# A tile's small product ahead of the next tile's transposes, two norm weights loaded as rows with the taps, and four raw buffers for the small columns

## The chip, the cores and the metric

The kernel runs on one core of one Trainium2 chip. The metric is device time in microseconds (us) of one execution; lower is better. Engines are named as the profile names them: PE (TensorE matmuls and transposes; PEld its weight loads), DVE (VectorE), ACT (ScalarE), POOL (GpSimd), SP (the queue that issues most DMAs).

## The reference

One layer of a hybrid decoder block, float32, on 1024 tokens of width 1024. Only what the change touches is followed closely below: the norm of the input, the narrow ("small") columns of the input projection, and the two norm weights of the sparse attention.

```python
h = rms_norm(x, norm_mix)                          # x (1024, 1024)
proj = h @ w_in                                    # w_in (1024, 3020)
qkv, z, a_g, b_g, c_q, c_kv, k_idx, w_idx, ug = split_cols(proj, IN_SPLITS)
y_a = gdn_mixer(qkv, z, a_g, b_g, ...)             # causal conv of 4 taps, gated delta rule in chunks
y_b = dsa_mixer(c_q, c_kv, k_idx, w_idx, ..., dsa_q_norm, dsa_k_norm)   # top-k sparse attention
y_c = conv_mixer(ug, ...)                          # causal conv of 31 taps, layer norm
x = x + concat([y_a, y_b, y_c]) @ w_out
x = x + memory_cross_attention(rms_norm(x, norm_cross), rms_norm(mem, norm_mem), ...)
x = x + square(relu(rms_norm(x, norm_mlp) @ mlp_w1)) @ mlp_w2
```

The 460 columns 2048 to 2507 of `w_in` (`a_g`, `b_g`, `c_q`, `c_kv`, `k_idx`, `w_idx`) are the small columns. In the sparse attention q and k are normed over 64 columns with the weights `dsa_q_norm` and `dsa_k_norm`, 64 numbers each.

## The kernel before

Tokens are worked in eight tiles of 128 rows. A float32 product is made from three products of rounded parts (`mm3`, L130 to L135): each operand is split into a high part, cast to fp32r, and a low part, the difference. `unit` (L170) loads a piece of a weight into a raw buffer, casts the high part on ACT or POOL and subtracts for the low part on DVE or POOL (L184). `split` (L142 to L145) does the same for an activation: the cast on ACT, the difference on DVE.

The program begins with `norm_small` (L290), and this is the part that the change is about. Four units of the small columns' weight are loaded (`ws`, two blocks of 128 rows of `w_in` each, here called u0 to u3); their raw buffers are the shared `wraw`, of which there are two. For u0 and u2 the low part is made on DVE, for u1 and u3 on POOL. Then a software pipeline runs over the tiles: at turn i it norms tile i (`rms_rows`: the squares and their sum on ACT, then a chain of ten short DVE instructions for the inverse root, L156 to L168; `norm_rows`: one DVE instruction of 1024 columns, L195), transposes tile i-1 on PE and splits it into `hT` (`rows_T`, 8 transposes, two casts on ACT, two differences on DVE), multiplies tile i-2 by the small columns (24 PE instructions of 460 columns into one bank of PSUM, then copies out), and does three later steps for tiles i-3, i-4 and i-5 (transposes of the small columns, `prep_tile`, `prep_queries`). The loads of x go into a pool of three buffers.

Written order is not final order: the program is built with a scheduler that moves instructions within each engine's queue by its own estimate of times. An engine then takes its queue strictly in order. So a change near the start can change the order of instructions far behind it.

`taps` (L681) gathers the convolutions' taps and two norm weights as rows of one tile and transposes it once on PE. `prep_keys` (L462), called after it, loads `dsa_q_norm` and `dsa_k_norm` as columns with four DMAs of 64 rows of one number and multiplies the two on DVE (`gqkc`, L472). After `norm_small` follow `ug_stage` (PE products of the columns of the convolution), the index scores and the top-k search, the qkv products with their convolution, the z gate, then a weave of the memory's keys and values (`mem_stage`, tiles `mkv`), the convolution's norm (`cyc`) and the first chunk of the delta rule (`gdn_pre`, `gdn_blocks`, `gdn_post`, tiles `gp`, `Tb`/`Wb`, `gi`), a weave of the eight chunks with the sparse attention (`da`), cross attention, and the MLP, which takes the second half of the time.

## Time and profile before

| | |
|---|---|
| median of three runs | 1643.58 us (1643.33 to 1648.39) |
| the profiled execution's own time | 1641.49 us |
| its span, from the first to the last instruction | 1639.7 us |
| busy share of the span | PE 93%, PEld 77%, DVE 72%, ACT 45%, POOL 20% |
| chain that ended last, by engine | PE 60%, DVE 18%, ACT 10%, issue 6%, DMA 4%, POOL 2% |
| mean granted TensorE clock | 0.963 of full speed |

Times in all rows count from the start of the span. The chain that ended last is followed back from the last instruction: at each step to what released it. A busy PE is not a PE at its peak.

### The profile page before, as it was taken

How to read it: one execution, taken by the hardware profiler on the slowest of the kernel's cores; microseconds unless marked ns; L12 is line 12 of the kernel's file. 1: busy time of each engine (PE TensorE's matmuls, PEld its weight loads, DVE VectorE, ACT ScalarE, POOL GpSimd, SP SyncE). 2: the span in 40 equal slices, each digit the busy share in tenths (PEclk: the TensorE clock that was granted, in tenths of full speed). 3: DMA queues.
4: the chain of work that ended last, by engine and by line, in shares of the span. 5: the costliest groups of instructions: out<-in, count | busy, mean ns of one | idle time of the engine just before them, and what ended most of it. 6: DMA issues, size and time to landing. Idle time of an engine off the chain costs nothing.

```text
span 1639.7 us, 20580 instructions
## 1 busy us (share of the span) xinstructions
PE 1519.0 (93%) x7497; PEld 1265.0 (77%) x7497; DVE 1174.4 (72%) x2149; ACT 740.2 (45%) x1483; POOL 322.4 (20%) x297
## 2 busy tenths in 40 slices
PE   6999999997985789999889997999999999999998
PEld 5977888885775678889777885788888888888887
DVE  7649868778158598886756878997569656965783
ACT  4535777883541456655434524433234223323331
POOL 3021434345355233221401104100000000000000
PEclk9999999998987799999999998999999999999999
DMA  5130121221543434322831347733560364146202
GB/s 188 58 99 19 44 62 52 78 71 43 158 138 110 145 103 124 100 72 82 293 112 39 123 173 272 307 113 116 196 227 26 131 231 177 52 154 238 96 7 97
DMA packets 114123, 201.93 MB, mean 123 GB/s; under 512 B 15469, under 2 KB 64358, under 8 KB 106854
## 3 DMA queue, kind: packets, MB, share of 16 engines
q1 hardware_dynamic: 112486, 195.37, 34.7%
q0 software_dynamic: 1536, 5.24, 0.9%
q8 instruction: 59, 0.97, 0.2%
q14 instruction: 42, 0.34, 0.1%
HBM read 150.26 MB, written 50.33 MB: 122 GB/s over the span
## 4 chain that ended last, share of the span: by engine, by line
PE 60%; DVE 18%; ACT 10%; issue 6%; DMA 4%; POOL 2%; SPq 0%; ACTq 0%; DVEq 0%; POOLq 0%
PE mlp_mm L135 12%; PE mlp_mm L134 12%; PE mlp_mm L133 12%; ACT junka L591 5%; DVE acc L739 1%; DVE bm L1454 1%; PE xw_mm L135 1%; PE xw_mm L134 1%; PE xw_mm L133 1%; PE xq_mm L135 1%; PE xq_mm L133 1%; DVE tk_t L599 1%; PE xq_mm L134 1%; DVE junk L593 1%; DVE Tb L994 1%
## 5 line engine op out<-in xcount | busy, mean ns | idle before, releaser
L134 PE MATMUL mlp_mm<-bm,wm 128*128 128x512 f32 x448 | 178.3, 398 | 5.9 <-DVE bm L1454 5.9
L135 PE MATMUL mlp_mm<-bm,wm 128*128 128x512 f32 x448 | 178.1, 398 | 0.3 <-DVE wm L1454 0.3
L133 PE MATMUL mlp_mm<-bm,wm 128*128 128x512 f32 x448 | 176.7, 397 | 1.2 <-ACT bm L1453 1.2
L134 PE MATMUL mlp_mm<-wm,am 128*128 128x512 f32 x448 | 176.9, 395 | 0.0
L135 PE MATMUL mlp_mm<-wm,am 128*128 128x512 f32 x448 | 176.9, 395 | 0.0
L133 PE MATMUL mlp_mm<-wm,am 128*128 128x512 f32 x448 | 175.0, 395 | 0.0
L1453 ACT CAST wm<-wq 128x2048 fp32r<-128x2048 f32 x32 | 61.2, 1911 | 212.2 <-PE mlp_mm L134 212.0
L1543 DVE TENSOR_TENSOR xacc<-xacc,mlp_mm 128x512 f32<-128x512 f32 x112 | 75.8, 682 | 69.5 <-PE mlp_mm L135 69.5
L134 PEld LDWEIGHTS mlp_mm<-bm,wm 128*128 128x128 f32 x448 | 84.8, 189 | 27.1 <-DVE bm L1454 6.7
L133 PEld LDWEIGHTS mlp_mm<-bm,wm 128*128 128x128 f32 x448 | 84.6, 189 | 21.8 <-ACT bm L1453 1.4
L135 PEld LDWEIGHTS mlp_mm<-bm,wm 128*128 128x128 f32 x448 | 84.9, 189 | 21.1 <-DVE wm L1454 0.8
L133 PEld LDWEIGHTS mlp_mm<-wm,am 128*128 128x128 f32 x448 | 84.2, 188 | 20.3
L134 PEld LDWEIGHTS mlp_mm<-wm,am 128*128 128x128 f32 x448 | 84.2, 188 | 20.2
L135 PEld LDWEIGHTS mlp_mm<-wm,am 128*128 128x128 f32 x448 | 84.2, 188 | 20.2
L1454 DVE TENSOR_TENSOR wm<-wsum,wm 128x2048 fp32r<-128x2048 f32 x24 | 58.2, 2427 | 52.3 <-ACT wm L1453 52.3
L1454 DVE TENSOR_TENSOR wm<-wq,wm 128x2048 fp32r<-128x2048 f32 x32 | 73.3, 2291 | 28.5 <-ACT wm L1453 28.4
L1453 ACT CAST wm<-wsum 128x2048 fp32r<-128x2048 f32 x24 | 45.9, 1912 | 105.9 <-PE mlp_mm L134 76.5
L1507 ACT ACTIVATE aq<-mlp_mm 128x512 f32<-128x512 f32 x64 | 37.9, 596 | 68.8 <-PE mlp_mm L135 68.6
L184 POOL TENSOR_TENSOR wlo<-wraw,whi 128x1024 fp32r<-128x1024 f32 x28 | 68.4, 2443 | 1.8
L133 PE MATMUL cv_mm<-Y,diag 128*128 128x512 f32 x124 | 50.2, 405 | 10.4 <-POOL diag L782 10.4
L591 ACT ACTIVATE junka<-negm,tk_cand 128x384 bf16<-128x384 int16 (+1 forms) x68 | 52.6, 774 | 15.1 <-DVE tk_cand L600 13.7
L591 ACT ACTIVATE junka<-lo,tk_cand 128x384 bf16<-128x384 uint16 (+1 forms) x64 | 49.5, 773 | 18.5 <-DVE tk_cand L600 12.5
(511 smaller groups left out, 4119.2 us busy)
## 6 DMA issues: line engine op xcount, KB each, us to landing
bm<-hb_d SPq DMA_DIRECT2D x42, 1024.0 KB, 5.8
wq<-in_mlp_w SPq DMA_DIRECT2D x32, 1024.0 KB, 5.3
hb_d<-bm SPq DMA_DIRECT2D x14, 1024.0 KB, 5.0
wraw<-in_w_in SPq DMA_DIRECT2D x20, 512.0 KB, 3.7
qkv_d<-acc SPq DMA_DIRECT2D x12, 512.0 KB, 3.2
x<-in_x SPq DMA_DIRECT2D x8, 512.0 KB, 6.4
gnx<-qkv_d SPq DMA_DIRECT2D x8, 512.0 KB, 3.9
wraw<-in_xa_wkv SPq DMA_DIRECT2D x8, 512.0 KB, 4.4
```

Source lines behind the costliest of these rows:

```text
L133: mm(out, l[0], r[0], start=start, stop=False, skip_group_check=on)
L134: mm(out, l[0], r[1], start=False, stop=False, skip_group_check=on)
L135: mm(out, l[1], r[0], start=False, stop=stop, skip_group_check=on)
L184: (lo_eng or nc.gpsimd).tensor_sub(lo[:, :n], raw[:, :n], hi[:, :n].bitcast(F32))
L591: Sc.activation(junka[:, :K], X[b], AF.Sign, bias=c, scale=-1.0, accum_out=n)
L593: V.tensor_scalar(junk[:, :K].bitcast(X[b].dtype), X[b], c, None, op0=OP.is_lt, op1=OP.add, accum_out=n)
L599: V.tensor_tensor(t, cnt, th, op=OP.is_le)
L739: nc.vector.scalar_tensor_tensor(acc, xb[:, 3 - d:3 - d + T], self.cw[:, 3 - d, i:i + 1], acc, op0=OP.mult, op1=OP.add)
L1453: Sc.copy(w[0], x)
L1454: V.tensor_sub(w[1], x, w[0].bitcast(F32))
L1507: Sc.activation(x, ps[ch, m], AF.Relu if c == "21" else AF.Copy)
L1543: V.tensor_add(x, x, ps[ch, tt])
```

## The change

Three edits. The two raw buffers that u2 and u3 had to share with u0 and u1 are no longer needed: u2 and u3 load into one `whi` and one `wlo` buffer of the same pool, and the loads of x tiles 1 and 2 are placed after u1 and after u3. In a turn of the pipeline the small product (of tile i-2) is written ahead of the transposes (of tile i-1). And the two attention norm weights become two more rows of the taps' tile, so the four column loads and their tile go away.

```diff
-        raw = (rpool or pool).tile([P, rcap or cap], F32, name=rtag or tag + "raw", bufs=raw_bufs)
+        rtag = rtag or tag + "raw"
+        raw = (rpool or pool).tile([P, rcap or cap], F32R if rtag in ("whi", "wlo") else F32, name=rtag, bufs=raw_bufs).bitcast(F32)
...
-                               rpool=wu, rtag="wraw", rcap=1024, hi_act=True, lo_eng=nc.vector if u % 2 == 0 else None))
-            if u < 2:
-                load(u + 1)
+                               rpool=wu, rtag=("wraw", "wraw", "whi", "wlo")[u], rcap=1024, hi_act=True, lo_eng=nc.vector if u % 2 == 0 else None))
+            if u == 1:
+                load(1)
+        load(2)
...
-            t = i - 1
-            if 0 <= t < NT:
-                self.stage = "n1"
-                sl = slice(t * P, (t + 1) * P)
-                self.rows_T(ys.pop(t), *((lambda q, m=m: m[:, q * 4:q * 4 + 4, sl]) for m in hT))
             t = i - 2
             if 0 <= t < NT:
                 self.stage = "small"
...
                 nc.vector.tensor_copy(ga[:, t, 8:12], ps[:, 456:460])
+            t = i - 1
+            if 0 <= t < NT:
+                self.stage = "n1"
+                sl = slice(t * P, (t + 1) * P)
+                self.rows_T(ys.pop(t), *((lambda q, m=m: m[:, q * 4:q * 4 + 4, sl]) for m in hT))
...
-        gc = pool.tile([P, 2], F32, name="gqc")
-        for j, nm in enumerate(("dsa_q_norm", "dsa_k_norm")):
-            for s in range(2):
-                src = A[nm]
-                nc.sync.dma_start(gc[s * 64:(s + 1) * 64, j:j + 1],
-                                  bass.AP(tensor=src.tensor, offset=src.offset, ap=[[1, 64], [1, 1]]))
+        gc = self.gqk
...
-        rows = pool.tile([121, P], F32, name="taprows")
+        rows = pool.tile([123, P], F32, name="taprows")
...
+        for i, nm in enumerate(("dsa_q_norm", "dsa_k_norm")):
+            src = A[nm]
+            nc.sync.dma_start(rows[121 + i:122 + i, :].rearrange("p (s n) -> p s n", s=2),
+                              bass.AP(tensor=src.tensor, offset=src.offset, ap=[[64, 1], [0, 2], [1, 64]]))
```

What the scheduler makes of it is seen in the queues. SP, from the program's start: the names are tiles with their buffer numbers; the four 128x2x460 loads are u0 to u3, the 128x1024 loads of `in_x` are the tiles of x. Before:

```order
L302 DMA x1_119<-in_x 128x1024
L140 DMA g1_121<-in_norm_mix 128x1024
L179 DMA wraw_123<-in_w_in 128x2x460
L302 DMA x1_129<-in_x 128x1024
L179 DMA wraw_131<-in_w_in 128x2x460
L302 DMA x1_137<-in_x 128x1024
...
L302 DMA x1_286<-in_x 128x1024
L469 DMA gqc_1124<-in_dsa_k_norm 64x1
L179 DMA wraw_139<-in_w_in 128x2x460
...
L179 DMA wraw_145<-in_w_in 128x2x460
```

After:

```order
L303 DMA x1_119<-in_x 128x1024
L140 DMA g1_121<-in_norm_mix 128x1024
L180 DMA wraw_123<-in_w_in 128x2x460
L180 DMA wraw_129<-in_w_in 128x2x460
L303 DMA x1_135<-in_x 128x1024
L180 DMA whi_137<-in_w_in 128x2x460
L180 DMA wlo_143<-in_w_in 128x2x460
L303 DMA x1_149<-in_x 128x1024
```

u1 moved ahead of x tile 1, u2 and u3 from far behind the taps to the places ahead of x tile 2, which goes from sixth to eighth.

PE, from the program's start: `n1_y_168`, `n1_y_188` and `n1_y_222` are the normed tiles 0, 1 and 2, of each of which four transposes at a time go into a bank; `small_mm` is the product, whose 24 rows are cut to the first and the last. Before:

```order
L202 MATMUL n1_mm_215<-ident_66,n1_y_168 128x128 x4
L202 MATMUL n1_mm_242<-ident_66,n1_y_188 128x128 x4
...
L133 MATMUL small_mm_256<-wshi_124,hT0_104 128x460
...
L135 MATMUL small_mm_256<-wshi_146,hT1_105 128x460
L202 MATMUL n1_mm_308<-ident_66,n1_y_222 128x128 x4
...
L133 MATMUL small_mm_322<-wshi_124,hT0_104 128x460
```

After:

```order
L203 MATMUL n1_mm_215<-ident_66,n1_y_168 128x128 x4
L133 MATMUL small_mm_242<-wshi_124,hT0_104 128x460
...
L135 MATMUL small_mm_242<-wshi_144,hT1_105 128x460
L203 MATMUL n1_mm_272<-ident_66,n1_y_188 128x128 x4
...
L133 MATMUL small_mm_308<-wshi_124,hT0_104 128x460
L134 MATMUL small_mm_308<-wslo_125,hT0_104 128x460
L203 MATMUL n1_mm_338<-ident_66,n1_y_222 128x128 x4
...
L350 MATMUL small_mm_352<-ident_66,sm_267 128x128 x4
L135 MATMUL small_mm_308<-wshi_124,hT1_105 128x460
```

Tile 0's whole product now stands ahead of tile 1's transposes; the first two instructions of tile 1's product stand ahead of tile 2's transposes, the other 22 behind them.

From the end of `norm_small` to the weave of memory and first chunk, some 390 us on, the queues of PE and POOL hold the same instructions in the same order; from there to the end of the sparse attention the scheduler's order differs again, and the MLP's is the same. POOL in that weave (`whi`, `wlo` are the parts of a unit of the memory's weight, `XT` begins the first chunk's `gi` steps). Before:

```order
L184 TENSOR_TENSOR wlo<-wraw,whi 128x1024
L833 TENSOR_TENSOR cyc<-cyc,conv_ln_b 128x1024
L183 TENSOR_SCALAR whi<-wraw 128x1024
L184 TENSOR_TENSOR wlo<-wraw,whi 128x1024
L183 TENSOR_SCALAR whi<-wraw 128x1024
L184 TENSOR_TENSOR wlo<-wraw,whi 128x1024
L1245 DMA gz<-gz_d 128x512 x2
L967 MEMSET Wb 32x272
L1014 TENSOR_TENSOR XT<-xc,bm 128x512
```

After:

```order
L835 TENSOR_TENSOR cyc<-cyc,conv_ln_b 128x1024 x2
L185 TENSOR_TENSOR wlo<-wraw,whi 128x1024
L184 TENSOR_SCALAR whi<-wraw 128x1024
L185 TENSOR_TENSOR wlo<-wraw,whi 128x1024
L1247 DMA gz<-gz_d 128x512 x2
L969 MEMSET Wb 32x272
L184 TENSOR_SCALAR whi<-wraw 128x1024
L1016 TENSOR_TENSOR XT<-xc,bm 128x512
L970 MEMSET Wb 32x16
L185 TENSOR_TENSOR wlo<-wraw,whi 128x1024
```

SP's queue keeps this weave's instructions but moves the last unit's load (`wraw<-in_xa_wkv`) from ahead of a `yc_d` store and the second load of `Ab` to just behind them. The last unit's two instructions moved from ahead of the clearing of `Wb` to either side of `XT`; in PE's queue 22 of that unit's products now stand between the first chunk's `gi_mm<-X,NAT` and its `gi_mm<-Z,XT`, where none stood.

## Rows read from the trace of the kernel before

**Rows 1.** Busy time by stretch: the stretch, its length, then for each engine busy us and, in brackets, instructions; then the granted PE clock, the DMA engines' mean busy share and GB/s.

```profile
27.00:76.00 49.00, 49.00 (x297) 45.13 (x295) 35.22 (x112) 24.86 (x63) 8.38 (x7) 1.00 0.29 92
76.00:87.00 11.00, 7.92 (x56) 6.76 (x54) 8.06 (x24) 9.51 (x28) 0.23 (x2) 0.93 0.34 100
560.00:780.00 220.00, 200.48 (x1426) 180.83 (x1425) 177.82 (x571) 134.36 (x351) 56.14 (x68) 0.98 0.32 98
```

**Rows 2.** Timeline of the first 28 us, PE: start, duration, engine, line, operation, output and input, shapes; in brackets how long the engine sat idle before it and what ended that.

```profile
16.49 1.97 PE L202 MATMUL n_mm<-ident,n_y 128*128 128x128 f32 x8 [5.48 <-DVE rs_i L158]
...
19.03 0.59 PE L135 MATMUL small_mm<-wshi,hT 128*128 128x460 f32 x1
19.41 0.59 PE L133 MATMUL small_mm<-wshi,hT 128*128 128x460 f32 x1
...
20.99 0.37 PE L135 MATMUL small_mm<-wshi,hT 128*128 128x460 f32 x1
21.20 0.37 PE L133 MATMUL small_mm<-wshi,hT 128*128 128x460 f32 x1
...
24.34 0.48 PE L134 MATMUL small_mm<-wslo,hT 128*128 128x460 f32 x1 [0.90 <-POOL wslo L184]
...
26.34 1.09 PE L202 MATMUL n_mm<-ident,n_y 128*128 128x128 f32 x8 [0.69 <-DVE rs_x L156]
```

**Rows 3.** Timeline of SP's queue: the issues of u1, u2 and u3 (the duration is that of the issue, not of the transfer).

```profile
2.70 0.43 SPq L179 DMA_DIRECT2D wraw<-in_w_in  x1
...
14.21 0.53 SPq L179 DMA_DIRECT2D wraw<-in_w_in  x1
...
15.37 0.53 SPq L179 DMA_DIRECT2D wraw<-in_w_in  x1
```

**Rows 4.** Timeline of ACT: the squares of x tile 1, the cast of u1, the two casts of tile 0's `hT`, the casts of u2 and u3.

```profile
9.15 1.06 ACT L191 ACTIVATE n_y<-x 128x1024 f32<-128x1024 f32 x1 [0.36 <-DMA x<-in_x]
...
10.41 0.96 ACT L181 CAST wshi<-wraw 128x920 fp32r<-128x920 f32 x1
...
11.28 1.06 ACT L144 CAST hT<-n_mm 128x512 fp32r<-128x512 f32 x2
...
19.39 0.96 ACT L181 CAST wshi<-wraw 128x920 fp32r<-128x920 f32 x1 [5.91 <-DMA wraw<-in_w_in]
...
21.09 0.96 ACT L181 CAST wshi<-wraw 128x920 fp32r<-128x920 f32 x1 [0.26 <-DMA wraw<-in_w_in]
```

**Rows 5.** Timeline of DVE and POOL in the same stretch; the last two rows are the first of the ten short instructions of a later tile and the norm that follows them.

```profile
11.45 2.13 POOL L184 TENSOR_TENSOR wslo<-wraw,wshi 128x920 fp32r<-128x920 f32 x1 [8.69 <-ACT wshi L181]
11.47 2.12 DVE L164 TENSOR_TENSOR rs_t<-rs_y 128x1 f32<-128x1 f32 x1
...
19.92 0.16 DVE L472 SCALAR_TENSOR_TENSOR gqkc<-gqc 128x1 f32<-128x1 f32 x1 [3.41 <-issue]
...
20.65 1.12 DVE L184 TENSOR_TENSOR wslo<-wraw,wshi 128x920 fp32r<-128x920 f32 x1
...
25.01 1.28 DVE L195 SCALAR_TENSOR_TENSOR n_y<-x,n_y,g 128x1024 f32<-128x1024 f32 x1
...
25.25 2.17 POOL L184 TENSOR_TENSOR wqblo<-wraw,wqbhi 128x512 fp32r<-128x512 f32 x1
...
31.54 0.14 DVE L156 TENSOR_SCALAR rs_x<-n_ss 128x1 f32<-128x1 f32 x1
...
33.46 1.28 DVE L195 SCALAR_TENSOR_TENSOR n_y<-x,n_y,g 128x1024 f32<-128x1024 f32 x1
```

**Rows 6.** Timeline at the end of `norm_small`: PE's last small product, ACT's cast of a later step, and PE's last wait before `ug_stage`.

```profile
76.11 0.37 PE L135 MATMUL small_mm<-wshi,hT 128*128 128x460 f32 x1
...
76.95 0.37 ACT L144 CAST CQ<-small_mm 128x256 fp32r<-128x256 f32 x1
...
86.00 1.12 PE L456 MATMUL prep_mm<-ident,qd 128*128 128x128 f32 x4 [1.43 <-ACT qd L445]
```

**Rows 7.** Timeline of the weave of memory and first chunk, PE, DVE and POOL: the last unit's split on POOL and two DVE instructions beside it, the last step of `gdn_blocks` on DVE, `XT` on POOL, and the first `gi` steps on PE and DVE.

```profile
512.70 1.16 POOL L183 TENSOR_SCALAR whi<-wraw 128x1024 fp32r<-128x1024 f32 x1
512.85 1.01 DVE L163 SCALAR_TENSOR_TENSOR rs_y<-rs_t,rs_i 128x4 f32<-128x4 f32 x1
...
513.94 2.34 POOL L184 TENSOR_TENSOR wlo<-wraw,whi 128x1024 fp32r<-128x1024 f32 x1
514.02 2.37 DVE L994 TENSOR_TENSOR Tb<-Wb,Pb 32x64 f32<-32x64 f32 x1
...
524.24 0.66 DVE L996 TENSOR_REDUCE Wb<-Tb 32x64 f32<-32x512 f32 x1
...
530.18 1.29 POOL L1014 TENSOR_TENSOR XT<-xc,bm 128x512 f32<-128x512 f32 x1 [2.38 <-DMA xc<-Xb_d]
...
533.56 1.16 PE L1027 MATMUL gi_mm<-X,NAT 128*128 128x128 f32 x8 [0.68 <-ACT X L1020]
...
537.17 0.70 DVE L1028 COPY_PREDICATED Z<-mask,gi_mm 128x512 f32<-128x512 int32 x1
...
537.93 2.08 PE L1033 MATMUL gi_mm<-Z,XT 128*128 128x128 f32 x8 [3.21 <-DVE Z L1028]
```

**Rows 8.** Busy time by stretch as in rows 1 (without POOL), of the instructions on the tiles `mkv_mm` alone.

```profile
525.00:529.00 4.00, 4.00 (x20) 4.00 (x20) 0.69 (x1) 0.59 (x1) 0.50 0.65 219
529.50:532.00 2.50, 2.50 (x23) 2.50 (x23) 0.42 (x1) 0.37 (x1) 1.00 0.42 136
```

**Rows 9.** DMA issues of the memory's weight: output and input, queue, operation, count, KB each, median us from issue to landing.

```profile
wraw<-in_xa_wkv SPq DMA_DIRECT2D x8, 512.0 KB, 4.4
```

**Rows 10.** Timeline of SP's queue in the weave: the issue of the last unit's load and of the second load of `Ab`.

```profile
506.94 0.37 SPq L179 DMA_DIRECT2D wraw<-in_xa_wkv  x1
...
520.85 0.33 SPq L966 DMA_DIRECT2D Ab<-Ab_d  x1
```

More of the change, by code (lines that the diff above doesn't have):

```diff
@@ L689, in taps @@
         nc.sync.dma_start(rows[113:121, :], A["norm_mem"].rearrange("(i p) -> i p", p=P))
-        pt = self.mm_ps([P, 121])
-        nc.tensor.transpose(pt, rows, self.ident[0:121, 0:121])
-        tp = C.tile([P, 121], F32, name="taps")
+        for i, nm in enumerate(("dsa_q_norm", "dsa_k_norm")):
+            src = A[nm]
+            nc.sync.dma_start(rows[121 + i:122 + i, :].rearrange("p (s n) -> p s n", s=2),
+                              bass.AP(tensor=src.tensor, offset=src.offset, ap=[[64, 1], [0, 2], [1, 64]]))
+        pt = self.mm_ps([P, 123])
+        nc.tensor.transpose(pt, rows, self.ident[0:123, 0:123])
+        tp = C.tile([P, 123], F32, name="taps")
         nc.vector.tensor_copy(tp, pt)
@@ L698, in taps @@
         self.gmc = tp[:, 113:121]
+        self.gqk = tp[:, 121:123]
     def ug_stage(self, wu, wp, hT, Y):
```

## The prediction

> **What bounds the kernel now.** I read the busy time by stretch first, then the timelines of PE, DVE, ACT, POOL and SP over the first 28 us, then those of the places where the queues' order changes. From 27 to 76 us PE is busy for all of 49.00 us, so in that stretch nothing is won by a faster helper: it ends when it began plus its own work [rows 1]. It begins with tile 2's transposes at 26.34 [rows 2]. Ahead of them PE is starved, as the brackets say: 5.48 us before tile 1's transposes, 0.90 us at 24.34 for POOL's low part of u3, 0.69 us at 26.34 for DVE's root of tile 2 [rows 2]. The reason for the 0.90 us is in SP's queue: u1 goes out at 2.70, u2 and u3 at 14.21 and 15.37 [rows 3], and ACT's casts of u2 and u3 start at 19.39 and 21.09, the first after 5.91 us of idleness that ends with the DMA [rows 4]. DVE is hindered by POOL: a root step on 128x1 elements starts at 11.47, POOL's `wslo` at 11.45, and they end within 0.01 us of each other, 2.12 and 2.13 us long; ten such steps otherwise take 1.92 us together, from 31.54 to 33.46 [rows 5]. DVE also idles for 3.41 us ahead of `gqkc` [rows 5]. From 76 to 87 us PE works 7.92 us of 11 and ACT 9.51, so there ACT's order counts [rows 1].
>
> In the weave of the memory and the first chunk `XT` waits 2.38 us for the DMA of `xc`, and PE then 3.21 us for `Z` [rows 7]. From 560 to 780 us PE is busy 200.48 of 220 us [rows 1].
>
> **The change, part by part.** *Four raw buffers.* The transfers' spacing I take from ACT: x tile 1 is there at 9.15, u1 at 10.41 at the latest [rows 4], so 1.26 us for each tile that follows. u1 takes x tile 1's place and lands at about 9.15, x tile 1 at 10.41, u2 at 11.7, u3 at 12.9, x tile 2 at 14.2. In ACT's queue then stand the square of tile 1 (1.06, to 11.6), tile 0's casts (1.06, to 12.7), the casts of u2 and u3 (0.96 each, to 14.6), the square of tile 2 (to 15.9) [rows 4]. u2's cast is thus some 6 us earlier than now. POOL splits u1 from 10.1 to 12.2 and u3 from about 14.9 to 17.0, by 2.13 us each; DVE splits u2 (1.12) from 13.8 to 14.9 [rows 5]. From 14.9 DVE has tile 1's root, and I assume that its last steps again stand still beside POOL, until 17.0; with about half of 1.92 us left they end at 18.2 and the norm of tile 1 (1.28) at 19.5 [rows 5]. If POOL's `wqblo` starts first, it is 20.6: that instruction took 2.17 us beside a norm that it overlapped for 1.04 us, from 25.25 to 26.29, so its own work is 1.13 [rows 5]. Tile 2 then takes nine short steps (nine tenths of 1.92, 1.7) and 1.28: 22.5 to 23.7. I take 23.6, the late end, because the one lock that the rows show lasted the whole POOL instruction.
>
> The Trainium skill, "SBUF — State Buffer", section "SBUF: two separate sides", says that DVE and GpSimd share one pair of ports under an exclusive lock, so that a DVE instruction with two SBUF inputs stands still for a whole GpSimd one that reads SBUF; the trace agrees (2.12 beside 2.13 us). By that rule the change brings POOL's splits into DVE's root chain; without the lock the norm of tile 1 would end at about 17.4 instead of 19.5.
>
> *Order of product and transposes.* PE can start tile 0's product once both casts and u1's low part are there, at about 12.7. Its 24 products are spaced 0.38 us early on (19.03 to 19.41) and 0.21 us later (20.99 to 21.20) [rows 2]: 5 to 9 us, done by 17.7 to 21.8. Tile 1's transposes need the norm at 19.5 to 20.6, so the product mostly hides in PE's former idleness and does not hold tile 2. The gain at the beginning of the dense stretch is 26.34 − 23.6 = 2.7 us; two products of tile 1 that now stand ahead of tile 2's transposes are off the stretch behind them, 2 × 0.21 = 0.4. **−3.1**, with bounds of −4.2 (tile 2 at 22.5) and −1.8 (one more POOL split of 1.13 us or so in DVE's way).
>
> *Norm weights as rows.* Four loads and `gqkc` go. The 3.41 us idle ahead of `gqkc` lies on DVE while PE has u3's low part to wait for, so taking it away pays only through the chain above: 0 by itself. The two rows come with the taps, whose transposes stand behind the dense stretch: 0, and if one such load were late, one DMA's latency, of the order of 4.4 us by the only one in the rows [rows 9]; a load from the first microseconds has over 50 us of cover.
>
> *The end of `norm_small`.* After its last product at 76.11 PE's next long wait is 1.43 us for `qd` of ACT at 86.00 [rows 6]. In ACT's queue of the changed kernel three casts, the one of `CQ` (0.37) among them [rows 6], come ahead of a copy that waits for the last product: between 0 and two of those casts, 0.7. I take **−0.5**.
>
> *The weave.* POOL's two last splits leave DVE's way there: beside them DVE instructions took 1.01 us on 128x4 elements and 2.37 us on 32x64 [rows 7], 3.4 us together. They are in the chain to `Wb` and from there by a DMA to `XT`, or not; hence `XT` ends at 531.5 as now (530.18 + 1.29) or at 528.1. From its end to the end of `gi_mm<-X,NAT` (533.56 + 1.16 = 534.72) it is 3.2 us [rows 7], so 531.3 to 534.7. Then come 22 products of the last unit before `gi_mm<-Z,XT`: at 2.50/23 = 0.11 us each with the granted clock at 1.00, 2.4 us; at 4.00/20 = 0.20 with it at 0.50, 4.4 us [rows 8]. `Z`'s copy (0.70) fits into that. `gi_mm<-Z,XT` starts, instead of at 537.93, at 533.7 to 535.7 with the stall gone, or at 537.1 to 539.1 with nothing gained: −4.2 to +1.2. No row tells which, so I take the middle, **−1.5**.
>
> *From 560 us on.* The scheduler's order differs again. PE leaves 19.5 us idle in 220 [rows 1]; a tenth or so of it either way, ±2, and 0 in the sum, since no row favours a sign.
>
> The sum: −3.1 − 0.5 − 1.5 = −5.1. The profiled execution took 1641.49 us with a span of 1639.7; so the profile after would show about 1636.4 (span 1634.6). The median is 2.1 above the profiled execution; on it the sum gives 1643.58 − 5.1 = **1638.5**.
>
> **The rivals.** *All of it comes.* DVE has no late lock (tile 2 at 22.5), the whole 3.4 us reaches `Z`, and the products there run at full clock: −4.2 − 0.7 − 4.2 = −9.1, 1634.5. For it: all 3.4 us lie on DVE ahead of its last step at 524.24. Against it: 8 us pass between, and `XT` is freed by a DMA.
>
> *Only the beginning stays.* One more split holds tile 2 (−1.8), and in the weave the 22 products at half clock take what it gains (+0.2 to +1.2): −1.6 to −0.6 in the worst case, about −2 with the tail: 1641.5.
>
> *Nothing.* POOL's splits hold DVE until 26 us, as now, so that four earlier loads merely turn a wait for u3 into one for the root; the weave gives +1.2: 1643 to 1645. For it: 0.69 us of today's wait at 26.34 is for DVE already [rows 2]. Against it: the inputs are 6 us earlier.
>
> *Slower.* The last unit's load stands behind the second load of `Ab`, issued at 520.85 instead of 506.94 [rows 10]. With 4.4 us to land [rows 9] it is there at 525.6, `whi` (1.16) done at 526.8, ahead of `XT` at 530.18 by 3.4 us. But `whi` now stands in front of `XT` on POOL: were the load late, the first chunk would wait. To turn the gain of 3.6 elsewhere into a loss of 4.9 it takes 8.5 + 3.4 = 12 us more lateness; 1649 or more. Against it: the longest such time that the rows give is 4.4.
>
> **How the numbers follow.** What a measurement of this kernel tells from no change is about 0.3%, 4.9 us: faster is below 1638.65, slower above 1648.5. The forecast, −3 to −6.5 (1637.1 to 1640.6), 0.50; all of it 0.14 (1633 to 1637); only the beginning 0.17 (1640.6 to 1642.5); nothing 0.13 (1642.5 to 1646); slower 0.06. Faster gets 0.14 and somewhat over half of the forecast, 0.42; slower 0.06; same the rest, 0.52. The range leaves out the far end of the first rival, of the third, and the last one: 1634.0 to 1644.5.
>
> **What would show it.** Right: casts of u2 and u3 at 12 to 15 us; no wait for `gqkc`; tile 2's transposes at 23 to 24 and PE dense from there; the stretch ends some 3 us earlier, and `qd`'s wait at 86 comes about 3.6 us earlier. In the weave `XT` at 527 to 530 and `gi_mm<-Z,XT` ahead of 538 less what was won before. Wrong: u2 landing after 14 us, a DVE instruction of the root that lasts as long as a POOL split beside it around 20 to 25 us, tile 2 at 26; `whi` ahead of `XT` waiting for its load; or a gain at 87 us that is gone by 780, which would put the scheduler's new order there in place of my 0.

## The result, and the profile after

The changed kernel takes 1629.86 us in the median of four runs (1625.15 to 1632.49), the kernel before 1645.05 in four (1643.33 to 1648.39): a ratio of 0.9918, interval 0.9894 to 0.9942, 15.2 us less. Run again on another occasion it took 1628.89 (ratio 0.9920, 0.9890 to 0.9950). Forecast were 5.1 us less and a range of 1634.0 to 1644.5: the sign was right, the size was not, and the time lies 4.1 us below the range.

Two executions of the changed kernel are profiled (1631.19 and 1627.70 us) and two of the kernel before (1641.49, which the prediction read, and 1639.15). This table, made from PE's and DVE's timelines, holds where some stages begin, in us from the start of the span (the last row is a length: the MLP takes two fifths of the span, not half); "buffers" and "order, rows" are the first two experiments below. "That chain" is the run of dependent PE steps from `gi_mm<-Z,XT` on, which is shown further down.

| begin of | before | before, again | changed | changed, again | buffers | order, rows |
|---|---|---|---|---|---|---|
| tile 2's transposes | 26.34 | 26.90 | 23.55 | 23.55 | 26.49 | 24.21 |
| `ug_stage` on PE | 86.97 | 87.51 | 84.61 | 84.58 | 87.05 | 84.56 |
| memory's first product | 462.25 | 460.91 | 458.84 | 458.52 | 461.71 | 458.71 |
| last step of `Wb` (DVE) | 524.24 | 524.22 | 516.12 | 519.67 | 521.63 | 523.04 |
| first `gi_mm<-Z,XT` | 537.93 | 538.22 | 529.83 | 533.47 | 535.90 | 538.48 |
| `gp_mm<-ident,Lk` behind that chain | 553.65 | 553.02 | 540.48 | 544.24 | 546.65 | 554.19 |
| first `gs_mm` | 562.77 | 559.17 | 547.13 | 550.84 | 553.59 | 562.69 |
| MLP's first product | 991.92 | 989.09 | 974.85 | 978.44 | 983.47 | 991.76 |
| MLP, first to last product | 643.52 | 644.00 | 650.84 | 643.57 | 642.91 | 643.51 |

The stretch in which PE is always busy (the dense stretch) begins 2.8 us earlier. Timeline of the changed kernel, PE: tile 1's and tile 2's transposes, the last small product, the wait for `qd` and the first product of `ug_stage`; they answer to [rows 2, 6].

```profile
19.46 1.04 PE L203 MATMUL n_mm<-ident,n_y 128*128 128x128 f32 x8
...
23.55 1.97 PE L203 MATMUL n_mm<-ident,n_y 128*128 128x128 f32 x8 [2.14 <-DVE n_y L196]
...
75.02 0.40 PE L135 MATMUL small_mm<-wshi,hT 128*128 128x460 f32 x1
...
84.05 0.66 PE L458 MATMUL prep_mm<-ident,qd 128*128 128x128 f32 x4 [1.25 <-ACT qd L447]
84.54 0.27 PE L692 MATMUL taps_mm<-ident,taprows 123*128 123x123 f32 x1
84.61 0.47 PE L133 MATMUL ug_mm<-hT,whi 128*128 128x512 f32 x1
```

Tile 1's transposes no longer wait; tile 2's still do, for DVE's norm. And they take 1.97 us where they took 1.09 [rows 2]. The first 3 us of the dense stretch, of the kernel before and then of the changed one, tell why (columns as in [rows 1]; the granted clock is third from the end):

```profile
26.30:29.30 3.00, 2.96 (x18) 2.73 (x19) 2.65 (x11) 2.12 (x4) 1.85 (x3) 1.00 0.63 176
```

```profile
23.50:26.50 3.00, 2.95 (x13) 2.95 (x14) 2.83 (x11) 1.53 (x3) 0.01 (x1) 0.51 1.13 344
```

Behind its wait of 2.14 us PE begins the stretch at half the clock, 1.2 instead of 2.4 GHz, and so the last small product is only 1.1 us earlier (75.02 against 76.11 [rows 6]). That is not so in every execution. Eight of the profiles kept here have all three edits at the beginning. In four of them, both of the changed kernel among them, the clock is near 0.50 for some 3 us there, and `ug_stage` begins at 84.58 to 85.01; in the other four it stays at 1.00, and `ug_stage` begins at 82.80 to 83.24, though tile 2 starts at 23.39 to 23.87 in all eight. The length of PE's wait ahead of it (1.74 to 2.14 us in the first four, 1.55 to 2.56 in the others) does not decide which, and no run shows what does.

DVE and POOL of the changed kernel show what tile 2 waits for, and answer to [rows 5]:

```profile
14.70 2.12 DVE L163 SCALAR_TENSOR_TENSOR rs_y<-rs_t,rs_i 128x1 f32<-128x1 f32 x1
...
20.55 1.22 DVE L166 SCALAR_TENSOR_TENSOR rs_t<-rs_s 128x1 f32<-128x1 f32 x1
...
22.21 1.28 DVE L196 SCALAR_TENSOR_TENSOR n_y<-x,n_y,g 128x1024 f32<-128x1024 f32 x1
...
14.58 2.22 POOL L185 TENSOR_TENSOR wslo<-wlo,wshi 128x920 fp32r<-128x920 f32 x1 [2.09 <-ACT wshi L182]
...
20.48 1.27 POOL L185 TENSOR_TENSOR wqblo<-wraw,wqbhi 128x512 fp32r<-128x512 f32 x1
```

Two root steps of 128x1 elements stand still until the POOL split beside them ends (16.82 and 16.80 us; 21.77 and 21.75).

In the weave of memory and first chunk, POOL and DVE and then PE, against [rows 7]:

```profile
519.51 1.03 POOL L184 TENSOR_SCALAR whi<-wraw 128x1024 fp32r<-128x1024 f32 x1
521.03 1.25 POOL L1016 TENSOR_TENSOR XT<-xc,bm 128x512 f32<-128x512 f32 x1 [0.49 <-DMA xc<-Xb_d]
...
522.29 2.34 POOL L185 TENSOR_TENSOR wlo<-wraw,whi 128x1024 fp32r<-128x1024 f32 x1
...
516.12 0.67 DVE L998 TENSOR_REDUCE Wb<-Tb 32x64 f32<-32x512 f32 x1
...
522.89 0.69 DVE L145 TENSOR_TENSOR kvt<-mkv_mm,kvt 128x512 fp32r<-128x512 f32 x1 [5.44 <-DMA v_d<-kvt]
...
526.24 0.73 DVE L1030 COPY_PREDICATED Z<-mask,gi_mm 128x512 f32<-128x512 int32 x1 [0.29 <-PE gi_mm L1029]
```

```profile
524.13 2.07 PE L1029 MATMUL gi_mm<-X,NAT 128*128 128x128 f32 x8 [0.68 <-ACT X L1022]
...
528.13 0.42 PE L135 MATMUL mkv_mm<-whi,mT 128*128 128x256 f32 x1
...
529.71 0.28 PE L135 MATMUL mkv_mm<-whi,mT 128*128 128x256 f32 x1
529.83 1.05 PE L1035 MATMUL gi_mm<-Z,XT 128*128 128x128 f32 x8
531.56 0.66 PE L1041 MATMUL gi_mm<-ident,X 128*128 128x128 f32 x4 [0.68 <-ACT X L1037]
...
540.48 0.66 PE L907 MATMUL gp_mm<-ident,Lk 128*128 128x128 f32 x4 [0.68 <-ACT XT L1047]
```

`gi_mm<-Z,XT` has no bracket any more, for two reasons. `Z` comes sooner behind `gi_mm<-X,NAT`: in the kernel before, a subtraction that waits for a store (`kvt`, for `v_d`) stands between the two on DVE,

```profile
536.39 0.69 DVE L145 TENSOR_TENSOR kvt<-mkv_mm,kvt 128x512 fp32r<-128x512 f32 x1 [1.47 <-DMA v_d<-kvt]
```

and in the changed one that wait is over at 522.89, ahead of `X,NAT`. What is left of the wait for `Z` is 0.82 us, as experiment 9 shows, in which the products are left out; the products fill it and last some 3 us longer. They also raise the clock: `X,NAT` still runs at the lower level (2.07 us, against 1.16 before), the products take 0.42 us each at first and 0.28 at the end, and `Z,XT` takes 1.05 us where it took 2.08 [rows 7]. From there to `gp_mm<-ident,Lk` the chain of seven steps, most of which wait for the one before by way of ACT or DVE, takes 10.65 us (529.83 to 540.48); before it took 15.72 (537.93 to 553.65). The busy time of that chain, first of the kernel before, then of the changed one (columns as in [rows 1]; the figure that counts is the granted clock, third from the end):

```profile
538.00:554.00 16.00, 12.10 (x50) 10.68 (x51) 5.69 (x10) 2.93 (x5) 1.69 (x3) 0.50 0.60 186
```

```profile
530.00:540.50 10.50, 6.26 (x49) 5.38 (x48) 5.61 (x8) 3.88 (x7) 1.70 (x3) 1.00 0.70 219
```

The same work, at 1.2 GHz there and at 2.4 GHz here. This is 5.1 us. It is no chance of one execution: the chain takes 14.80 to 15.72 us in the two profiles of the kernel before and in those of experiments 2, 3, 4 and 7, which have its order, and 10.65 to 10.92 in the two of the changed kernel and in those of experiments 1, 12, 13 and 14, which have the changed order.

In the first profile of the changed kernel 7.3 us are lost again in the MLP, in the second not (last row of the table). The first split of `bm` on DVE and the first sum on POOL (and, for the changed kernel, the PE product that waits for the split), in the kernel before, in the changed one, and in the changed one again:

```profile
1002.37 2.29 DVE L1454 TENSOR_TENSOR bm<-h,bm 128x2048 fp32r<-128x2048 f32 x1
...
1002.96 6.13 POOL L1412 TENSOR_TENSOR wsum<-wq 128x2048 f32<-128x2048 f32 x1 [58.53 <-DMA wq<-in_mlp_w]
```

```profile
986.55 6.58 DVE L1456 TENSOR_TENSOR bm<-h,bm 128x2048 fp32r<-128x2048 f32 x1
...
986.02 4.96 POOL L1414 TENSOR_TENSOR wsum<-wq 128x2048 f32<-128x2048 f32 x1 [58.67 <-DMA wq<-in_mlp_w]
...
993.19 0.80 PE L134 MATMUL mlp_mm<-bm,wm 128*128 128x512 f32 x1 [8.65 <-DVE bm L1456]
```

```profile
988.74 2.29 DVE L1456 TENSOR_TENSOR bm<-h,bm 128x2048 fp32r<-128x2048 f32 x1
...
989.57 5.88 POOL L1414 TENSOR_TENSOR wsum<-wq 128x2048 f32<-128x2048 f32 x1 [58.60 <-DMA wq<-in_mlp_w]
...
991.08 0.80 PE L134 MATMUL mlp_mm<-bm,wm 128*128 128x512 f32 x1 [4.77 <-DVE bm L1456]
```

Whichever starts first makes the other wait: POOL started 0.53 us ahead in the changed kernel's first profile, DVE 0.83 ahead in its second. PE's wait is 8.65 us in the one case and 4.77 in the other. So single executions of one kernel spread by several us, and a profile's total is not the median.

### The profile page after: what moved, and what is told of

The parts are those of the page before. It is cut to its first block, busy times and chain, and to the rows that moved or that the text cites. A ratio compares the mean times of both kernels' runs of the same rounds, so it can differ in the third digit from the quotient of the medians.

```text
span 1629.4 us, 20582 instructions
## 1 busy us (share of the span) xinstructions
PE 1508.6 (93%) x7497; PEld 1256.2 (77%) x7497; DVE 1171.4 (72%) x2149; ACT 739.6 (45%) x1483; POOL 318.6 (20%) x297
## 4 chain that ended last, share of the span: by engine, by line
PE 65%; DVE 16%; ACT 9%; issue 5%; DMA 3%; POOL 1%; SPq 0%; ACTq 0%; DVEq 0%; POOLq 0%
PE mlp_mm L134 13%; PE mlp_mm L135 13%; PE mlp_mm L133 13%; ACT junka L588 5%; DVE acc L741 1%; PE gi_mm L1029 1%; PE xq_mm L133 1%; PE xq_mm L134 1%; PE xw_mm L135 1%; PE xw_mm L133 1%; PE xw_mm L134 1%; PE xq_mm L135 1%; DVE tk_t L596 1%; PE small_mm L135 1%; DVE junk L590 1%
## 5 line engine op out<-in xcount | busy, mean ns | idle before, releaser
L133 PEld LDWEIGHTS mlp_mm<-wm,am 128*128 128x128 f32 x448 | 84.1, 188 | 20.4
L134 PEld LDWEIGHTS mlp_mm<-wm,am 128*128 128x128 f32 x448 | 84.1, 188 | 20.4
L1456 DVE TENSOR_TENSOR wm<-wsum,wm 128x2048 fp32r<-128x2048 f32 x24 | 54.9, 2289 | 51.5 <-ACT wm L1455 51.5
L133 PE MATMUL cv_mm<-Y,diag 128*128 128x512 f32 x124 | 50.2, 405 | 11.2 <-POOL diag L784 11.2
```

Of the source, the lines that this page charges most:

```text
L133: mm(out, l[0], r[0], start=start, stop=False, skip_group_check=on)
L134: mm(out, l[0], r[1], start=False, stop=False, skip_group_check=on)
L1456: V.tensor_sub(w[1], x, w[0].bitcast(F32))
```

## The experiments

**1. The buffers alone.** Of the diff above only the three hunks on `raw`, `rtag` and the loads.

> Only the first edit (u2 and u3 in one whi and one wlo buffer, x tiles 1 and 2 loaded behind u1 and u3). In its POOL queue the last unit's split stands on either side of XT, as in the changed kernel. Theory A (the gain of 15 us is mainly the scheduler's new order in the weave of memory and first chunk, and the buffers bring it): 8 to 17 us faster than before, first chunk's gi_mm<-Z,XT at 528 to 533 us instead of 537.93, granted clock near 1.00 in the 10 us behind it. Theory B (the gain adds up from three edits, a part from each): 3 to 6 us faster. Tile 2's transposes start at 23.5 to 24.5 us by both.

1633.37 us, ratio 0.9932 (0.9910 to 0.9954). So the buffers alone bring some 12 us, where all three edits brought 15, and theory A holds for the size, but two of its marks were missed. PE's timeline, tile 1's and tile 2's transposes:

```profile
18.91 1.97 PE L203 MATMUL n_mm<-ident,n_y 128*128 128x128 f32 x8 [8.03 <-DVE rs_i L157]
26.49 1.03 PE L203 MATMUL n_mm<-ident,n_y 128*128 128x128 f32 x8
```

The loads come early, yet tile 2 starts at 26.49: PE does not begin the product until tile 1's transposes are through, and is then busy up to tile 2. And `gi_mm<-Z,XT` came at 535.90, not at 528 to 533. Most of the gain lies behind it: from there to `gp_mm<-ident,Lk` 10.75 us, against 15.72.

**2. Order and rows, without the buffers.**

> The second and third edits without the buffers. The weave keeps the order of before (last split ahead of the clearing of Wb). Theory A: within 3 us of before, since the weave is as it was; gi_mm<-Z,XT at 536 to 539 us, clock at 0.50 to 0.65 behind it. Theory B: 5 to 10 us faster. Tile 2's transposes at 25 to 26.5 us, since u3 still comes late.

1640.78 us, ratio 0.9970 (0.9954 to 0.9986): 4.7 us, between what the two theories said. Tile 2's transposes start at 24.21, earlier than expected, and `ug_stage` at 84.56, as in the changed kernel's profiles, without any of its early loads. The weave is that of before, and its chain takes 15.71 us. So the early gain is the other two edits', the weave's gain the buffers'; 12.1 and 4.7 us make 16.8, where the changed kernel's two measurements have 15.2 and 14.8. Where the 4.7 us stay its profile (1640.69 us) does not show: it is 3.5 us ahead of the kernel before's first profile at the memory's first product and 0.2 at the MLP's; 1.6 of this go where PE waits 4.77 us for `Z` instead of 3.21.

**3 and 4. Rows alone, order alone.**

> Only the third edit (norm weights as rows of the taps; no gqkc in DVE's queue). Theory C (the early gain is the removed gqkc wait, which stood in the middle of tile 2's root on DVE): tile 2's transposes at 24 to 24.7 us instead of 26.34, the dense stretch ends 1.5 to 2.5 us earlier, total 2 to 5 us faster than before. Theory D (it is the order of product and transposes): as before, tile 2's transposes at 26.3 us, total within 2 us.

> Only the second edit (the small product ahead of the next tile's transposes). Theory C: tile 2's transposes within 0.5 us of 26.34, total within 2 us of before. Theory D: at 24 to 24.7 us, 2 to 5 us faster.

1642.99 us, ratio 0.9992 (0.9971 to 1.0014), and 1643.98, ratio 1.0011 (0.9993 to 1.0030). Tile 2's transposes, rows alone and then order alone:

```profile
24.24 1.09 PE L202 MATMUL n_mm<-ident,n_y 128*128 128x128 f32 x8
```

```profile
25.73 1.09 PE L202 MATMUL n_mm<-ident,n_y 128*128 128x128 f32 x8 [1.65 <-DVE n_y L195]
```

Theory C is right about the start: without `gqkc` in the middle of tile 2's root, tile 2 is 2.1 us earlier; the order alone gives 0.6. But neither is seen at the end by itself: `ug_stage` begins 1.35 and 0.8 us earlier, and the totals, for which theory C had 2 to 5 us, show nothing. That both together give what neither gives alone is not shown, since the intervals of the rows alone and of both overlap (0.9971 to 1.0014 and 0.9954 to 0.9986).

**5 and 6. The products, and then POOL's split, put back ahead.** The changed kernel, in which only the scheduler is told to issue `gi_mm<-X,NAT` behind the last unit's products, and in the second also `XT` behind its `wlo` (`hold` keeps that unit's `wlo` and last product; the lines that set it are left out):

```diff
+                with (self.tc.issue_after(self.hold[1].ins) if n == 0 and k == 4 and h == 0 else ExitStack()):
                     mm(py[:, h], NAT[:, h], X[:, h], start=True, stop=True)
...
+        with (self.tc.issue_after(self.hold[0].ins) if n == 0 else ExitStack()):
             G.tensor_mul(XT.rearrange("p h (b i) -> p h b i", b=8), xc.to_broadcast([P, H, 8, 16]),
```

> The changed kernel, but the first chunk's gi_mm<-X,NAT is issued only behind all products of the memory's last unit, as before; POOL's order stays the changed one. Theory A1 (the 22 products behind X,NAT keep PE busy, so that the clock is granted in full for the chain that follows, and they hide the wait for Z): about 5 to 8 us slower than the changed kernel, clock 0.50 to 0.65 in the 15 us behind X,NAT. Theory A2 (only POOL's order counts, because XT comes earlier): within 2 us of the changed kernel.

> As the run before, and XT on POOL is issued only behind the last unit's wlo, so POOL has the order of before too, but the last load still goes out late. Theory A1: no worse than the run before by more than 3 us. Theory A2: 4 to 8 us slower than the changed kernel, XT at 525 us or later instead of 521.

1632.94 us, ratio 0.9921 (0.9897 to 0.9944), and 1630.87, ratio 0.9918 (0.9893 to 0.9942): so the first stands 3 to 4 us above the changed kernel's medians and the second 1 to 2, with intervals that overlap; for the first A1 had 5 to 8 and A2 within 2, for the second A2 had 4 to 8, and none of these came. A1's mark for the second (no worse than the first by more than 3 us) did. PE's timeline of the first of them:

```profile
533.58 1.05 PE L1031 MATMUL gi_mm<-X,NAT 128*128 128x128 f32 x8
535.87 1.16 PE L1037 MATMUL gi_mm<-Z,XT 128*128 128x128 f32 x8 [1.24 <-DVE Z L1032]
...
546.58 0.66 PE L908 MATMUL gp_mm<-ident,Lk 128*128 128x128 f32 x4 [0.68 <-ACT XT L1049]
```

The chain takes 10.71 us here too: the products now end right ahead of `X,NAT`, and the wait for `Z` is 1.24 us, not 3.21. So their place behind `X,NAT` is not needed; products just ahead of the chain and no long wait behind them did as well here. That is not enough each time: in the second kernel, with a wait of 1.33 us, the clock fell in mid-chain (12.46 us). What decides between these two no run shows.

**7 and 8. The wait for `Z`, filled or taken away, in the kernel before.** First eight products that nobody reads, behind `gi_mm<-X,NAT`:

```diff
+            if n == 0 and k == 4:
+                self.stage = "fill"
+                pf = self.mm_ps([P, H, P])
+                for h in range(8):
+                    mm(pf[:, h % H], NAT[:, h % H], X[:, h % H], start=True, stop=True)
+                self.stage = "gi"
             V.copy_predicated(Z, self.masks[k][:, None, :].to_broadcast([P, H, P]), py)
```

> The kernel before, and eight idle products of 128x128 (the first chunk's X against NAT into a spare bank, never read) behind the first gi_mm<-X,NAT, where PE waits 3.21 us for Z. Nothing else moves. Theory A1 (the wait lets the clock fall, and the chain from gi_mm<-Z,XT to gp_mm<-ident,Lk then takes 15.7 us at 1.2 GHz instead of 10.6 at 2.4): granted clock 1.00 behind Z,XT, that chain 10.5 to 12 us, total 3 to 6 us faster than before. Rival: clock 0.50 there all the same, total within 2 us.

1643.72 us, ratio 1.0001 (0.9985 to 1.0016). Nothing, as the rival had it:

```profile
537.37 1.95 PE L1032 MATMUL fill_mm<-X,NAT 128*128 128x128 f32 x16
542.25 2.07 PE L1039 MATMUL gi_mm<-Z,XT 128*128 128x128 f32 x8 [2.93 <-DVE Z L1034]
```

1.95 us are filled, but `Z,XT` starts 5.87 us behind `X,NAT` where it was 4.37, so PE still waits 2.93, and the clock falls. The 1.5 us are not the filling's: three profiles with the order of before and no filling (experiments 2, 3 and 4) have 5.91 to 5.93 us, as here the rows alone:

```profile
535.28 1.16 PE L1027 MATMUL gi_mm<-X,NAT 128*128 128x128 f32 x8 [0.68 <-ACT X L1020]
541.20 2.07 PE L1033 MATMUL gi_mm<-Z,XT 128*128 128x128 f32 x8 [4.76 <-DVE Z L1028]
```

DVE's wait for the store of `v_d` lasts 3.02 us there instead of 1.47. So with this order there is a shorter and a longer wait for `Z`, and both profiles of the kernel before have the shorter one. Then two buffers for `kvt` (`bufs=2` in its two allocations), so that its subtraction ahead of `Z`'s copy has no store to wait for:

> The kernel before with two buffers for kvt, so that its subtraction ahead of Z's copy in DVE's queue does not wait for the store of v_d. Theory A1: Z is copied within 1.5 us of gi_mm<-X,NAT's end, PE's wait for it falls from 3.21 to about 1.3 us, the clock stays at 1.00, and the chain takes 10.6 us: 4 to 8 us faster than before. Rival: another wait takes its place, within 2 us.

1641.07 us, ratio 0.9971 (0.9950 to 0.9991), 2.8 us:

```profile
535.71 1.16 PE L1033 MATMUL gi_mm<-Z,XT 128*128 128x128 f32 x8 [1.28 <-DVE Z L1028]
537.54 0.86 PE L1039 MATMUL gi_mm<-ident,X 128*128 128x128 f32 x4 [0.68 <-ACT X L1035]
...
541.01 2.05 PE L1033 MATMUL gi_mm<-Z,XT 128*128 128x128 f32 x8 [0.91 <-DVE Z L1028]
```

The wait is 1.28 us as expected, and `Z,XT` starts 2.2 us earlier at the full clock; one step later the clock falls all the same. The chain takes 14.53 us instead of 15.72. 4 to 8 us were expected and 2.8 came, since the clock was not kept.

**9 and 10. Products left out, and more of them put in.** The changed kernel without 22 of the 24 products; then the kernel before with 24 filling products instead of eight (`range(24)` in the diff above).

> The changed kernel without 22 of the 24 products of the memory's last unit (one product for each of its two tiles is left; so part of the memory's values is left out, and PE has nothing to do between gi_mm<-X,NAT and gi_mm<-Z,XT). POOL's order is the changed one. Theory A3 (those products keep PE busy ahead of the chain, and so the chain from gi_mm<-Z,XT to gp_mm<-ident,Lk runs at 2.4 GHz): without them it takes 13 to 16 us instead of 10.6, with a granted clock near 0.50, though 2.5 to 4.7 us of work are gone. Rival (the clock there hangs on something else, such as the earlier arrival): 10.6 us, and the first chunk 1 to 3 us earlier still.

> The kernel before with 24 idle products of 128x128 behind the first gi_mm<-X,NAT instead of eight, so that they cover the whole wait for Z. Theory A3: the clock is 1.00 behind them, the chain from gi_mm<-Z,XT takes 10.6 to 12 us instead of 15.7; as the idle products themselves end 1 to 2 us behind Z, gp_mm<-ident,Lk comes 2 to 4 us earlier than in the kernel before, and the total is 1 to 4 us shorter. Rival: chain 15 us or more, total 0 to 3 us longer.

Left out, chain and clock:

```profile
529.36 2.08 PE L1039 MATMUL gi_mm<-Z,XT 128*128 128x128 f32 x8 [0.82 <-DVE Z L1034]
...
545.28 1.12 PE L911 MATMUL gp_mm<-ident,Lk 128*128 128x128 f32 x4 [0.68 <-ACT XT L1051]
```

```profile
530.00:545.00 15.00, 11.18 (x47) 9.77 (x46) 6.64 (x14) 3.29 (x6) 0.30 (x1) 0.50 0.75 237
```

15.92 us, at 0.50. The wait for `Z` is only 0.82 us, and the clock is at half all the same. With less work the chain is 5.3 us longer, as theory A3 has it, and the whole kernel is not faster for it (1631.74 us, ratio 0.9918, 0.9888 to 0.9948; 1.9 and 2.9 us above the changed kernel's medians, with intervals that overlap). From `X,NAT` to the first `gs_mm` it takes 26.03 us, the changed kernel with all its products 23.00. With 24 filling products in the kernel before:

```profile
535.51 5.52 PE L1032 MATMUL fill_mm<-X,NAT 128*128 128x128 f32 x48
540.87 1.06 PE L1039 MATMUL gi_mm<-Z,XT 128*128 128x128 f32 x8
...
553.38 0.66 PE L905 MATMUL gp_mm<-ident,Lk 128*128 128x128 f32 x4 [0.68 <-ACT XT L1051]
```

1640.58 us, ratio 0.9974 (0.9955 to 0.9993): 3.7 us less for 5.52 us of work that nobody reads. The chain takes 12.51 us, somewhat more than the 10.6 to 12 expected: the granted clock is 1.00 for its first 6 us, below 0.60 for the next 4, then 1.00 again. The profiles to hold beside it are those in which `Z` came as late, of experiments 2, 3 and 4: from `X,NAT` to `gp_mm<-ident,Lk` they take 21.62 to 21.64 us, this one 18.86; to the first `gs_mm` 30.07 to 30.14, this one 25.02. So the clock, and not the waits alone, made the chain long.

**11. Both kernels again.** The profile of the changed one is in the table; its total (1628.89 us) and its MLP (643.57) came as expected.

> The changed kernel once more, for a second profiled execution beside the next run on the same chip: 1625 to 1633 us. If DVE's first bm<-h split of the MLP again overlaps POOL's wsum<-wq, it takes 6.6 us instead of 2.3 and the MLP is some 7 us longer than in the kernel before (650.8 against 643.5 us); if not, the MLP takes 643 to 645 us.

> The kernel before once more, for a second profile: if the profile of before that the prediction read was a lucky one, mkv and XT come 1 to 4 us later than there, 1643 to 1648 us in all; the chain behind gi_mm<-Z,XT again at clock 0.50.

The kernel before ran in 1639.15 us, faster than expected and than its own medians of 1643.65 to 1645.5 over these comparisons: both of its profiles are of its faster executions. In this one the clock came back before the chain's end:

```profile
538.22 2.08 PE L1033 MATMUL gi_mm<-Z,XT 128*128 128x128 f32 x8 [3.21 <-DVE Z L1028]
...
551.22 1.13 PE L1043 MATMUL gi_mm<-XT,Z 128*128 128x128 f32 x8 [0.92 <-DVE Z L1028]
```

14.80 us for the chain, and 6.15 from its end to the first `gs_mm` at a granted clock of 1.00, where the other profile has 9.12 at 0.66.

**12 and 13. POOL's sum held back in the MLP.** The changed kernel, with one column copied from `bm` ahead of the sum, so that POOL waits for that split: from the second `bm`, and in another kernel from the first (`blo` is the low part of that split; the lines that set it are left out).

```diff
+                if eng is self.nc.gpsimd:
+                    eng.tensor_copy(d[:, 0, 0:1], self.blo[:, 0, 0:1].bitcast(F32))
                 eng.tensor_add(d, q["21"], q["22"])
```

> The changed kernel, with POOL's first wsum<-wq of the MLP made to wait for the low part of bm by a one-column copy from it ahead of the sum. Theory: the two then never overlap, DVE's bm<-h takes 2.3 us, PE's wait for it falls from 8.65 us to about 4.4, and the MLP is 4 to 7 us shorter than the 650.8 us of the changed kernel's profile: 1624 to 1627 us. Rival (the sum only moves on and locks the next DVE instructions instead): within 2 us of the changed kernel.

> The changed kernel, with POOL's first wsum of the MLP made to wait for the low part of the first bm (the run before held it to the second bm, 17 us later, and so made the MLP longer). Theory: the first bm<-h split takes 2.3 us in every execution, the MLP 643 to 645 us, total 1624 to 1629 us. Rival: within 1 us of the changed kernel in the median, since only some executions lose that race.

Held to the second: 1639.77 us, ratio 0.9971 (0.9954 to 0.9988), some 10 us slower than the changed kernel, the MLP 654.1 us, since the sum began only at 1013.97 and everything behind it came late. Held to the first: 1631.88, ratio 0.9936 (0.9914 to 0.9957), the MLP 645.9. The split then takes 2.28 us, but the median is 2 to 3 us above the changed kernel's, where the rival had it within 1; the intervals overlap. The race cost one profiled execution 7 us; what it does to the median is not shown, since the hold itself makes the MLP 2.3 us longer than in the changed kernel's second profile.

**14. A candidate.** The changed kernel with two `kvt` buffers and the right hold.

> The changed kernel with two buffers for kvt and with POOL's first wsum of the MLP held behind the first bm, both together, as a candidate for a better kernel. The DVE wait of some 5 us for the store of v_d goes, which delays nothing that PE needs in the changed kernel's order: 1626 to 1630 us, so within 3 us of the changed kernel. Rival: the scheduler's order changes and gives back more: 1632 us or more.

1627.42 us (1626.22 to 1635.10), ratio 0.9901 (0.9865 to 0.9937). It came as expected. It is the lowest median of all, 1.5 to 2.4 us below the changed kernel's, but the intervals overlap, so a gain over it isn't shown.

## Why the prediction was wrong, point by point

**The beginning: right in size, wrong in cause.** Tile 2's transposes were forecast for 23.6 and came at 23.55; u2's cast (12.67) and the lock by POOL's `wslo` (2.12 us) came as summed. That 23.6 was met so closely is in part luck. It had `wqblo` hold tile 1's norm up to 20.6; that norm ended at 18.92, and `wqblo` held a step of tile 2's root instead (1.22 us). The sum has small slips too: from 17.0, half of 1.92 and 1.28 us lead to 19.2, not 19.5, and without the lock to 18.1, not 17.4. And the term was put under the four buffers, and *norm weights as rows* was priced at "0 by itself". The runs show the opposite: rows alone move tile 2 by 2.1 us, buffers alone by none. The sentence that failed is that PE had "u3's low part to wait for" while DVE idled ahead of `gqkc`: true of the product at 24.34, but behind it tile 2 waited for a root that `gqkc` had split in two [rows 5].

**Up to `ug_stage`:** forecast −3.6 (3.1 and 0.5), measured −2.4. The prediction let the dense stretch end "when it began plus its own work" and did not ask for the clock at which that work runs. In both profiles of the changed kernel it runs at half the clock for some 3 us at first, which costs about 1.5 us (an estimate: 3 us at 0.51 instead of 1.00). Behind the last small product PE takes 9.59 us instead of 10.86; some 0.7 of this is six instructions that now stand ahead of that product, so about 0.6 is left for ACT's order, where 0.5 was forecast. In the four profiles in which the clock stayed at 1.00, `ug_stage` begins 3.7 to 4.2 us earlier than the 86.97 of before, as forecast.

**The weave up to `gi_mm<-Z,XT`:** forecast −1.5, bounds −4.2 and +1.2. Less the lead with which the weave was entered, the two profiles give −4.7 and −0.7, the buffers alone −1.5. The term holds roughly, though −4.7 lies outside its bounds. The two profiles differ mainly by a root on DVE: its last step comes 16.8 and 20.4 us behind the weave's first product, where it came 19.1 behind it in the kernel before. That `Z`'s copy "fits into that" came true for a reason the prediction did not give: the wait of `kvt` that stood ahead of the copy had moved away.

**The step that failed is that the sum of the weave ended at `gi_mm<-Z,XT`,** as if what follows were moved unchanged. It was not: the chain behind it ran at half the clock before. That stood in the rows: `Z,XT` took 2.08 us for the eight products that `X,NAT` did in 1.16 [rows 7]. I used the two levels only to price the 22 products. The chain up to `gp_mm<-ident,Lk` is 5.1 and 5.0 us shorter in the two profiles of the changed kernel, and from there to the first `gs_mm` 2.5 us more went, for the same reason as far as the second profile of before tells (6.15 us with the clock back). These 7.5 us were in no term and in no rival; "all of it comes" had −9.1 without them. Against the second profile of before, in which the clock came back early, they are 3.6 us; against experiments 2, 3 and 4, with the order of before, 6.8 to 6.9.

**From 560 us on,** forecast 0 ± 2: from the first `gs_mm` to the MLP −1.4 and −1.6. Right; the 7.3 us that the MLP lost in one profile were in no term.

**What stays open.** Between the first profile of before and the second of the changed kernel 13.8 us are told (1641.49 to 1627.70). The medians differ by 15.2, and where the kernel before loses the 3.6 and 5.9 us by which its median of 1645.05 lies above its two profiled executions is not shown. The 1.5 us by which `Z` can come later (experiments 2, 3 and 4) are a candidate for a part.

**The rivals and the signs.** The slower one did not come: `whi` started at 519.51 and held `XT` up by nothing, as `xc` came at 521.03. One sign of being wrong did come, a root step on DVE that lasts as long as the POOL split beside it between 20 and 25 us (1.22 us at 20.55), and yet tile 2 was there at 23.55.

## What to carry to other kernels

When a change moves a dependent chain to another neighbourhood, ask what TensorE does just ahead of it and at which granted clock each step of the chain runs now: two rows with the same work and different durations are a term of the sum. Independent products ahead of such a chain can pay twice then, by filling a wait and by raising the clock, and taking them away can make the chain slower (15.92 instead of 10.65 us). A wait that lies inside a root or another serial chain on the helping engine is priced with the chain's end, not with who waited last; and a single edit that shows nothing may still be part of a gain, so the edits want testing in pairs. A start that comes earlier is worth its full time only if the clock behind it is the same: here 2.8 us were won at tile 2 and 1.1 were left at the last small product.

## What the hardware showed unexpectedly

TensorE's clock: with 24 filling products (5.52 us busy) ahead of the chain most of it ran at 1.00, with eight (1.95 us, and 2.93 us of waiting behind) all of it at 0.50; leaving 22 products out of the changed kernel put it at 0.50. The Trainium skill, "TensorE: Matmul & The Clock Gate", section "Part 1: The HAM clock gate", says that the clock follows how busy the engine has just been; the three runs agree.

The lock between DVE and POOL reaches far beyond the short steps: beside POOL's sum of 128x2048 a split of DVE took 6.58 us instead of 2.29. POOL's sum started 11.2 and 11.1 us behind the MLP's first product in the two profiles of the changed kernel, DVE's split 11.7 and 10.3 us behind it: so 1.4 us on DVE's side decided who was held. The Trainium skill, "SBUF — State Buffer", section "SBUF: two separate sides", says that the one that starts first keeps the shared ports for its whole instruction; the three executions shown agree. It was not tried to take the lock away.
